# Thirteen raw weight buffers, new first and last norm chains, and 256 columns of each lo part on GpSimd

## The chip, the core and the metric

The kernel runs on one core of a Trainium2 chip. The metric is the device time of one execution in microseconds (us), lower is better. Engines are named as in the profile: PE (TensorE matmul), PEld (its weight loads), DVE (VectorE), ACT (ScalarE), POOL (GpSimd), SP (the queue that issues the DMAs).

## What is computed

A decoder trunk of two layers for 256 tokens of width 1024, in float32. Each layer is a token mixer (latent attention, retention, block attention behind one input projection), a layer norm, a channel mixer, and a layer norm; before the first layer stands one more norm. The channel mixer of layer 0 is a dense SwiGLU, that of layer 1 has eight experts, of which each token takes two:

```python
x = layer_norm(x, ln_emb_g, ln_emb_b)
for l in range(DEPTH):
    mix = hybrid_mixer(x, ...)
    x = layer_norm(DN_ALPHA * x + mix, ln1_g[l], ln1_b[l])
    f = swiglu(x, ...) if l % 2 == 0 else moe_swiglu(x, router, w_gate, w_up, w_down)
    x = layer_norm(DN_ALPHA * x + f, ln2_g[l], ln2_b[l])
# moe_swiglu, for each of 8 experts (D = 1024, inner width 3584):
y = y + gates[:, e:e + 1] * ((silu(xt @ w_gate[e]) * (xt @ w_up[e])) @ w_down[e])
```

## The kernel before

All weights are read once from HBM, 352 MB of them for the experts. To keep float32 accuracy at the speed of the rounded format fp32r, each weight tile `raw` is **split**: ACT writes `whi`, the tile rounded to fp32r (line 151), and DVE writes `wlo = raw - whi` (line 153). Activations are split in the same way, and a product is the sum of hi*hi, hi*lo and lo*hi.

The expert stage fills the last two thirds of the time. It goes over experts `e` (8) and blocks `m` of 512 inner columns (7). One such **m-step** reads three weight blocks (gate, up, and the down block of the m-step before) of two 128x2048 tiles each: six tiles of 1 MB, six splits. An expert that got more than 64 tokens (and expert 0 always) takes the branch `heavy`, with three matmuls for each 128x512 piece of weights; the others are **light**: tokens hi and lo lie side by side in one weight load, and two matmuls do for a piece. A `fold` matmul adds the two halves afterwards. Which branch is taken is known only when the kernel runs.

The tiles land in a ring of buffers: pools `raws`, `raws2` and `raws3` hold the counts of 0, 1 and 2 in `ORDER` (eleven in all), and piece number `EARLY` goes once into a borrowed tile. SP issues the DMA of a tile as soon as the buffer that it takes is free, which is when ACT and DVE have read its last content. `whi` and `wlo` have three buffers each in this stage. ACT and DVE run ahead of PE as far as these allow.

Between the splits DVE has small work that reads PSUM: `hh` (silu times up, line 938), `wk` (lo part of the turned hidden block, line 957), and now and then copies for gather and scatter. Their place in DVE's row is fixed by `defer`, which counts splits. POOL does almost nothing in this stage: it copies the rows of the last norm's scale and shift to all partitions (`gb`, line 1027) in expert 7.

At the very end the last down block runs, its result is scaled, scattered and added to the residual (`ln_sum`), and the last norm follows: sums on DVE and ACT, a handful of one-column operations on POOL (`ln_stats`, lines 187 to 195), then the rows of the result (line 202). At the very start scale and shift of the first norm are loaded by two DMAs that broadcast a row to 128 partitions (512 KB written each).

```python
            for c in range(0, 2048, n):
                ...
                split(raw(o + c, n), n, nc.vector, [x[:, c:c + n] for x in t])
                dve[0] = last[1]
```

Of the kernel before, what the change touches and what calls it, by code (L numbers as in the profile page):

```python
# [18 lines left out]
P = 128  # L19
# [15 lines left out]
EARLY = 11  # L35
# [7 lines left out]
WS = (8,3)  # L43
FENT = ((0, None, 2), (1, None, SPL))
ORDER = (0, 0, 0, 0, 1, 1, 1, 1, 0, 0, 2)
# [28 lines left out]
M_UT = M_E8 + 8  # L74
M_ON = M_UT + 128
M_ALL = M_ON + 128

# [9 lines left out]
def trunk(ctx: ExitStack, tc: tile.TileContext, x, consts, mconsts, vecs, lnrows, w_in, w_uq, w_ukv, w_o,  # L87
# [12 lines left out]
    mc = cpool.tile([P, M_UT], F32, name="mc")  # L100
# [4 lines left out]
    utb = cpool.tile([P, P], BF16, name="utb")  # L105
    onb = cpool.tile([P, P], BF16, name="onb")
# [77 lines left out]
    def ln_stats(s):  # L184
        nc.vector.tensor_scalar(s[:, 5:6], s[:, 0:1], s[:, 1:2], -1.0 / D, ALU.add, ALU.mult)
        nc.vector.tensor_scalar(s[:, 6:7], s[:, 1:2], s[:, 0:1], 1.0 / D, ALU.subtract, ALU.mult)
        nc.gpsimd.tensor_tensor(s[:, 6:7], s[:, 6:7], s[:, 6:7], ALU.mult)  # L187
        nc.gpsimd.tensor_scalar(s[:, 7:8], s[:, 3:4], 1.0 / D, LN_EPS, ALU.mult, ALU.add)  # L188
        nc.gpsimd.tensor_tensor(s[:, 7:8], s[:, 7:8], s[:, 6:7], ALU.subtract)  # L189
# [39 lines left out]
    def mixer(l, pool, poolb, cst, xhi, xlo, xres, raw, rest):  # L229
# [90 lines left out]
        if l == 0:  # L320
            load(cst, consts)
            load(mc[:, M_IO:], mconsts[:, M_IO:M_UT])
            uo = load(pool.tile([P, 2, P], F32, tag="oa", name="uo"), mconsts[:, M_UT:])
            nc.gpsimd.tensor_copy(utb, uo[:, 0, :])
            nc.gpsimd.tensor_copy(onb, uo[:, 1, :])
# [312 lines left out]
    def moe(pool, raws2, raws3, r, gb, rw):  # L638
# [28 lines left out]
        nc.gpsimd.tensor_copy(fo[:, :, 0], ident.rearrange("p (a b) -> p a b", b=2)[:, :, 1])  # L667
        for tt in range(2):
            ln_stats(r[tt][1])
        lgs = []  # L670
        for tt in range(2):
            x1 = ya[tt]
            pw, nm = ln_norm(*r[tt], gb, t0[:, tt], x1)
            lt = bank(acc, "lgp")
# [49 lines left out]
        iota = mc[:, M_IO:M_IO + 128]  # L724
# [150 lines left out]
        def gate_up(e, m, xg, part=None, mid=None):  # L875
# [60 lines left out]
            def mult():  # L936
                with after(dve[0]):
                    nc.vector.tensor_tensor(hh, bs[1], hh, ALU.mult)
# [5 lines left out]
            return hh, (lambda: fold_in(bs[1], fls[1])), mult  # L944

        def turn(hh, n, o=0):
# [5 lines left out]
            def halves():  # L952
# [3 lines left out]
                with after(dve[0]):  # L956
                    nc.vector.tensor_tensor(ht[:, :, 1], bv, ht[:, :, 0].bitcast(F32), ALU.subtract)  # L957
# [7 lines left out]
        def down(e, m, ht, yb, fold_up=None, fe=None, hook=None):  # L965
# [3 lines left out]

            def heavy(js=range(4)):  # L970
                for j in js:
                    for n in range(2):
                        cs = slice(j % 2 * D + n * 512, j % 2 * D + n * 512 + 512)
                        mm3(yb[n], ht[:, j, 0], ht[:, j, 1], sp[j // 2][0][:, cs], sp[j // 2][1][:, cs], m == 0 and j == 0, m == FM - 1 and j == 3)

            def light():
                for j in range(4):
                    if j == 3 and fold_up and fe == e:
                        fold_up()
                    h2 = ht[:, j].rearrange("p a b -> p (a b)")[:, 0:256:2]  # L980
                    for n in range(2):
                        for i in range(2):
                            nc.tensor.matmul(yb[n], h2, sp[j // 2][i][:, j % 2 * D + n * 512:j % 2 * D + n * 512 + 512],  # L983
                                             start=(m == 0 and j == 0 and i == 0), stop=(m == FM - 1 and j == 3 and i == 1))
# [167 lines left out]
        for e in range(NE):  # L1152
            pr = e // 2
            for m in range(FM):
# [29 lines left out]
        t1 = x3(F32, "t1", (P, 2, D))  # L1184
        for tt in range(2):
            ln_stats(fsums[tt])
# [250 lines left out]
```

## Time and profile before

| | before |
|---|---|
| time, median of 3 runs | 1436.97 us (1433.45 to 1437.19) |
| the profiled execution's own time | 1434.8 us |
| its span, first to last instruction | 1432.9 us |
| PE busy | 1355.6 us (95%) |
| DVE busy | 1171.8 us (82%) |
| ACT busy | 999.5 us (70%) |
| POOL busy | 68.3 us (5%) |
| read from HBM | 426.76 MB |

Busy shares are means over stages with different limits. The span is 1.9 us shorter than the time of the same execution. A PE that is busy all the time need not be at its peak, since the ends of matmuls are modelled.

### The profile page before, as it was taken

To read this page: it belongs to the slowest core of one execution; us is meant where nothing else is said; L and a number is where in the kernel's file an instruction comes from. 1 tells how busy PE (TensorE), PEld (TensorE's weight loads), DVE (VectorE), ACT (ScalarE), POOL (GpSimd) and SP (SyncE) were. 2 spreads that over 40 slices of the span, in tenths; PEclk is the share of its full clock that TensorE was granted. 3 is DMA by queue.
4 is the path that set the end of the run, shared out by engine and by line. 5 is a ranking of instruction groups with operands and counts; after the bars stand their busy time and mean duration, and the time that the engine had idled before them with its cause. 6 is when DMAs were issued, how large, how long until landed. Compare 5 with 4: busy or idle time off the path is not lost. (4 is left out here: it accounts for less than half of the span.)

```text
span 1432.9 us, 18660 instructions
## 1 busy us (share of the span) xinstructions
PE 1355.6 (95%) x6927; PEld 1121.2 (78%) x6927; DVE 1171.8 (82%) x1258; ACT 999.5 (70%) x1074; POOL 68.3 (5%) x110
## 2 busy tenths in 40 slices
PE   8999999999999899989989999999999999999994
PEld 7987999997987688867666678866678888886663
DVE  6577654557576988899999998889998888888996
ACT  4564444444564777788888887788887777778883
POOL 3011000003011000000000000000000000000101
PEclk9999999999999999999999999999999999999997
DMA  7733455453534689999999999999999999999980
GB/s 284 271 136 118 177 192 191 177 180 127 181 146 191 227 335 369 365 364 405 409 405 411 419 400 344 350 359 394 412 418 372 338 357 347 344 366 362 376 341 31
DMA packets 63515, 429.49 MB, mean 300 GB/s; under 512 B 7058, under 2 KB 7570, under 8 KB 15268
## 3 DMA queue, kind: packets, MB, share of 16 engines
q1 hardware_dynamic: 63364, 427.81, 77.7%
q8 instruction: 83, 1.36, 0.4%
q14 instruction: 36, 0.29, 0.1%
q0 software_dynamic: 32, 0.03, 0.0%
HBM read 426.76 MB, written 1.05 MB: 299 GB/s over the span
## 5 line engine op out<-in xcount | busy, mean ns | idle before, releaser
L153 DVE TENSOR_TENSOR wlo<-raw,whi 128x2048 fp32r<-128x2048 f32 (+5 forms) x479 | 917.1, 1935 | 163.8 <-ACT whi L151 161.7
L151 ACT CAST whi<-raw 128x2048 fp32r<-128x2048 f32 (+4 forms) x482 | 772.5, 1618 | 257.5 <-PE gu L586 43.9
L908 PE MATMUL eg<-wlo,xg 128*128 128x512 f32 x448 | 185.8, 415 | 17.9 <-DVE wlo L153 13.9
L162 PE MATMUL eg<-whi,xg 128*128 128x512 f32 x448 | 179.6, 401 | 0.0
L907 PE MATMUL eg<-whi,xg 128*128 128x512 f32 x448 | 178.7, 399 | 0.0
L163 PE MATMUL eg<-wlo,xg 128*128 128x512 f32 x448 | 177.7, 397 | 0.6 <-DVE wlo L153 0.3
L164 PE MATMUL eg<-whi,xg 128*128 128x512 f32 x448 | 176.9, 395 | 0.0
L908 PEld LDWEIGHTS eg<-wlo,xg 128*128 128x128 f32 x448 | 84.0, 187 | 68.0 <-DVE wlo L153 52.7
L163 PEld LDWEIGHTS eg<-wlo,xg 128*128 128x128 f32 x448 | 87.0, 194 | 19.4 <-DVE wlo L153 3.6
L983 PE MATMUL y<-whi,wk 128*128 128x512 f32 x224 | 90.8, 405 | 11.5 <-DVE wk L957 9.8
L164 PEld LDWEIGHTS eg<-whi,xg 128*128 128x128 f32 x448 | 87.0, 194 | 17.5
L585 PE MATMUL gu<-xhi,whi 128*128 128x256 f32 x352 | 99.8, 283 | 0.1
L586 PE MATMUL gu<-xlo,whi 128*128 128x256 f32 x352 | 99.7, 283 | 0.2 <-DVE xlo L225 0.2
L162 PEld LDWEIGHTS eg<-whi,xg 128*128 128x128 f32 x448 | 87.2, 195 | 16.0
L983 PE MATMUL y<-wlo,wk 128*128 128x512 f32 x224 | 93.3, 416 | 6.7 <-DVE wlo L153 5.5
L587 PE MATMUL gu<-xhi,wlo 128*128 128x256 f32 x352 | 99.6, 283 | 0.0
L907 PEld LDWEIGHTS eg<-whi,xg 128*128 128x128 f32 x448 | 84.3, 188 | 14.2 <-ACT whi L151 0.5
L162 PE MATMUL y<-whi,wk 128*128 128x512 f32 x224 | 87.4, 392 | 0.4 <-ACT hh L932 0.3
L163 PE MATMUL y<-wlo,wk 128*128 128x512 f32 x224 | 87.5, 391 | 0.2 <-DVE wlo L153 0.2
L164 PE MATMUL y<-whi,wk 128*128 128x512 f32 x224 | 87.3, 390 | 0.0
L585 PEld LDWEIGHTS gu<-xhi,whi 128*128 128x128 f32 x352 | 67.5, 192 | 0.7 <-DVE xlo L225 0.3
L586 PEld LDWEIGHTS gu<-xlo,whi 128*128 128x128 f32 x352 | 67.5, 192 | 0.6 <-DVE xlo L225 0.4
(317 smaller groups left out, 2071.8 us busy)
## 6 DMA issues: line engine op xcount, KB each, us to landing
raw<-in_e_gate SPq DMA_DIRECT2D x112, 1024.0 KB, 7.1
raw<-in_e_up SPq DMA_DIRECT2D x110, 1024.0 KB, 6.9
raw<-in_e_down SPq DMA_DIRECT2D x108, 1024.0 KB, 6.9
raw<-in_ffn_gu SPq DMA_DIRECT2D x22, 1024.0 KB, 4.9
raw<-in_ffn_dn SPq DMA_DIRECT2D x11, 1024.0 KB, 4.6
raw<-in_w_in SPq DMA_DIRECT2D x10, 960.0 KB, 4.6
raw<-in_w_o SPq DMA_DIRECT2D x8, 1024.0 KB, 6.7
gb<-in_lnrows SPq DMA_DIRECT2D x8, 512.0 KB, 5.7
```

What stands on the lines that cost most here:

```text
L151: last[0] = nc.scalar.copy(hi[:, :n], src)
L153: last[1] = (eng or nc.vector).tensor_tensor(lo[:, :n], src, hi.bitcast(F32)[:, :n], ALU.subtract)
L162: nc.tensor.matmul(o, ahi, bhi, start=start, stop=False)
L163: nc.tensor.matmul(o, ahi, blo, start=False, stop=False)
L164: return nc.tensor.matmul(o, alo, bhi, start=False, stop=stop)
L585: nc.tensor.matmul(o, hi[:, cs], xhi[:, k, :], start=(g == 0 and k == 0), stop=False)
L586: nc.tensor.matmul(o, hi[:, cs], xlo[:, k, :], start=False, stop=False)
L587: nc.tensor.matmul(o, lo[:, cs], xhi[:, k, :], start=False, stop=(g == 1 and k == 7))
L907: nc.tensor.matmul(bs[g], x2, sp[k // 4][0][:, cs], start=(k == 0), stop=False)
L908: nc.tensor.matmul(bs[g], x2, sp[k // 4][1][:, cs], start=False, stop=(k == 7))
L983: nc.tensor.matmul(yb[n], h2, sp[j // 2][i][:, j % 2 * D + n * 512:j % 2 * D + n * 512 + 512], start=(m == 0 and j == 0 and i == 0), stop= ...
```

## The change

Four things, in the order of the program:

1. **First norm.** The two rows of scale and shift (8 KB) are loaded to one partition, and PE multiplies them by a column of ones (four 128x512 float32 matmuls, `gbp`), so that they stand on all partitions in PSUM. DVE reads them there for the first 128 tokens; ACT copies them to SBUF for the others. The router's weights are loaded on SP at the start, and two constant matrices of the router are computed on DVE and POOL instead of loaded.
2. **Buffers.** `ORDER` has thirteen entries, with two more for `raws2`; the room comes from the constants and from a smaller scratch area for DMA descriptors.
3. **Side part.** For each full split of the expert stage (2048 columns, 326 of them) DVE subtracts the first 1792 columns, POOL the last 256.
4. **The end.** The last down block goes over its output halves one after the other (`order`) instead of alternating; of its four half splits the third lo part waits for `hh`, the fourth for `wk`; four float32 matmuls (`kw`) are added. The one-column operations of the last norm move from POOL to DVE, but for the power.

```diff
-EARLY = 11
+EARLY = 13
+WL = (2, 2)
+SIDE = 256
-ORDER = (0, 0, 0, 0, 1, 1, 1, 1, 0, 0, 2)
+ORDER = (0, 0, 0, 0, 1, 1, 1, 1, 1, 1, 0, 0, 2)
...
-    def split(src, n, lo_eng=None, to=None):
+    def split(src, n, lo_eng=None, to=None, side=0):
...
-            last[1] = (eng or nc.vector).tensor_tensor(lo[:, :n], src, hi.bitcast(F32)[:, :n], ALU.subtract)
+            h = n - side
+            if side:
+                nc.gpsimd.tensor_tensor(lo[:, h:n], src[:, h:n], hi.bitcast(F32)[:, h:n], ALU.subtract)
+            last[1] = (eng or nc.vector).tensor_tensor(lo[:, :h], src[:, :h], hi.bitcast(F32)[:, :h], ALU.subtract)
...
-                split(raw(o + c, n), n, nc.vector, [x[:, c:c + n] for x in t])
+                split(raw(o + c, n), n, nc.vector, [x[:, c:c + n] for x in t], SIDE if n == 2048 else 0)
...
                     def hook():
-                        mult()
+                        i = mult()
+                        kw = bank(wps, "kw")
+                        keep_warm(kw, mc, WL[0])
                         h2.append(turn(hh, 0, 1024))
+                        keep_warm(kw, mc, WL[1])
+                        hold_splits(((), None, 2), ((), None, 1, i), ((), None, 1, turned[0]))
...
         for tt in range(2):
-            ln_stats(fsums[tt])
+            s, t = st[tt], t1[:, tt]
+            ln_stats(s, nc.vector)
+            nc.vector.tensor_scalar(s[:, 8:9], s[:, 4:5], 1.0 / D, s[:, 7:8], ALU.mult, ALU.add)
+            nc.gpsimd.tensor_tensor(s[:, 9:10], s[:, 8:9], mhalf[:, :1], ALU.pow)
+            nc.vector.scalar_tensor_tensor(t, ya[tt], s[:, 5:6], g, ALU.add, ALU.mult)
...
-            t = gb_load(0)
-            gb = [t[i // 2][:, (i % 2) * 512:(i % 2 + 1) * 512] for i in range(4)]
+            rows = load(x3(F32, "rows", (P, 2, D))[0:1], lnrows[0:2, :].rearrange("(o a) b -> o a b", o=1))
             load(xin[1], x[P:S, :])
...
+                nc.tensor.matmul(gb[i], ones, rows[:, i // 2, cs], start=True, stop=True)
+                nc.scalar.copy(t[i // 2][:, cs], gb[i])
```

Three places in the order of instructions carry the prediction. First, DVE's row in expert 1, which is light in this run (`ys` and `r` are the scaled result and its scatter-add, the branches are those of `heavy` and `light`). Before:

```order
L153 TENSOR_TENSOR wlo<-raw,whi 128x2048 x2
L957 TENSOR_TENSOR wk<-ht,wk 128x4x128
L863 UNCONDITIONAL_BRANCH
L153 TENSOR_TENSOR wlo<-raw,whi 128x2048 x2
L997 UNCONDITIONAL_BRANCH
L863 UNCONDITIONAL_BRANCH
L153 TENSOR_TENSOR wlo<-raw,whi 128x2048 x2
L938 TENSOR_TENSOR hh<-eg,hh 128x512
```

The same place now, and behind it POOL's row, which was empty here:

```order
L156 TENSOR_TENSOR wlo<-raw,whi 128x1792 x2
L968 TENSOR_TENSOR wk<-ht,wk 128x4x128
L872 UNCONDITIONAL_BRANCH
L156 TENSOR_TENSOR wlo<-raw,whi 128x1792 x2
L1011 UNCONDITIONAL_BRANCH
L872 UNCONDITIONAL_BRANCH
L156 TENSOR_TENSOR wlo<-raw,whi 128x1792 x2
L947 TENSOR_TENSOR hh<-eg,hh 128x512
```

```order
L872 UNCONDITIONAL_BRANCH
L155 TENSOR_TENSOR wlo<-raw,whi 128x256 x2
L1011 UNCONDITIONAL_BRANCH
L155 TENSOR_TENSOR wlo<-raw,whi 128x256 x2
L872 UNCONDITIONAL_BRANCH
```

DVE's row keeps its order, with shorter lo parts, and POOL gets one instruction for each of them. In the four light experts 15 to 20 of 42 lo parts (36 in expert 7) are followed on DVE by at least one instruction that reads PSUM.

Second, POOL's row where it broadcasts the rows of the last norm in expert 7; the `ISA` rows without names set POOL up for the broadcast and back. Before, and now:

```order
L1027 ISA
L1027 ISA gb<-row 128x1024 x2
L863 UNCONDITIONAL_BRANCH x14
L174 ISA
L174 TENSOR_SCALAR sums<-sums 128x1 x2
```

```order
L155 TENSOR_TENSOR wlo<-raw,whi 128x256
L1041 ISA
L1041 ISA gb<-row 128x1024
L872 UNCONDITIONAL_BRANCH
L155 ISA
L155 TENSOR_TENSOR wlo<-raw,whi 128x256 x3
L872 UNCONDITIONAL_BRANCH
L1041 ISA
L1041 ISA gb<-row 128x1024
L155 ISA
L155 TENSOR_TENSOR wlo<-raw,whi 128x256 x2
```

The two broadcasts now stand between side parts, and POOL is set up four times there instead of once.

Third, DVE's row at the end (the last two down blocks, `hh` and `wk` of the last m-step, the scaling of `y`, the sums). Before, and now:

```order
L153 TENSOR_TENSOR wlo<-raw,whi 128x1024 x3
L938 TENSOR_TENSOR hh<-eg,hh 128x512
L153 TENSOR_TENSOR wlo<-raw,whi 128x1024
L957 TENSOR_TENSOR wk<-ht,wk 128x4x128
L863 UNCONDITIONAL_BRANCH
L1004 SCALAR_TENSOR_TENSOR wk<-y,gs,wk 128x512 x2
L181 SCALAR_TENSOR_TENSOR r,sums<-r,sc 128x512 x4
```

```order
L156 TENSOR_TENSOR wlo<-raw,whi 128x1024 x2
L947 TENSOR_TENSOR hh<-eg,hh 128x512
L156 TENSOR_TENSOR wlo<-raw,whi 128x1024
L968 TENSOR_TENSOR wk<-ht,wk 128x4x128
L156 TENSOR_TENSOR wlo<-raw,whi 128x1024
L872 UNCONDITIONAL_BRANCH
L1018 SCALAR_TENSOR_TENSOR wk<-y,gs,wk 128x512
L184 SCALAR_TENSOR_TENSOR r,sums<-r,sc 128x512
L1018 SCALAR_TENSOR_TENSOR wk<-y,gs,wk 128x512
L184 SCALAR_TENSOR_TENSOR r,sums<-r,sc 128x512 x3
```

`hh` moves ahead of one lo part, `wk` ahead of another, and the first scatter-add ahead of the second scaling. On PE the four `kw` matmuls stand ahead of the branch of the last down block but one.

## Rows read from the trace of the kernel before

**Rows 1.** Stretches: busy us of PE, PEld, DVE, ACT, POOL (instructions); PE clock; DMA share; GB/s.
```profile
16.00:20.00 4.00, 1.63 (x7) 1.27 (x8) 4.00 (x3) 1.46 (x2) 2.22 (x1) 0.94 1.03 432
...
520.00:600.00 80.00, 80.00 (x364) 66.63 (x363) 69.00 (x42) 58.12 (x41) 0.00 (x0) 1.00 0.93 357
650.00:800.00 150.00, 136.96 (x583) 100.50 (x582) 149.40 (x102) 132.72 (x114) 0.00 (x0) 1.00 1.01 408
```
**Rows 2.** DVE by line and shape, 520 to 600 us: count, busy us, mean ns, idle before.
```profile
L153 DVE TENSOR_TENSOR wlo<-raw,whi 128x2048 fp32r<-128x2048 f32 x28 | 64.1, 2292 | 11.3 <-ACT whi L151 11.3
```
**Rows 3.** The same, 650 to 800 us.
```profile
L153 DVE TENSOR_TENSOR wlo<-raw,whi 128x2048 fp32r<-128x2048 f32 x60 | 134.4, 2280 | 0.6 <-ACT whi L151 0.6
L938 DVE TENSOR_TENSOR hh<-eg,hh 128x512 f32<-128x512 f32 x10 | 6.8, 681 | 0.0
```
**Rows 4.** Waits of the DMA queue, 650 to 800 us: total us, times, longest.
```profile
SPq L120 <- DVE wlo L153: 120.6, 56, 3.7
```
**Rows 5.** Instructions in order of time, expert 2: start us, us, engine, what.
```profile
701.81 3.72 ACT L151 CAST whi<-raw 128x2048 fp32r<-128x2048 f32 x2
...
703.95 8.89 DVE L153 TENSOR_TENSOR wlo<-raw,whi 128x2048 fp32r<-128x2048 f32 x4
```
**Rows 6.** The same, first projection: DVE and POOL.
```profile
12.96 1.03 DVE L153 TENSOR_TENSOR wlo<-raw,whi 128x832 fp32r<-128x832 f32 x1
...
16.49 2.22 POOL L153 TENSOR_TENSOR wlo<-raw,whi 128x832 fp32r<-128x832 f32 x1 [0.67 <-ACT whi L151]
16.83 2.77 DVE L153 TENSOR_TENSOR wlo<-raw,whi 128x832 fp32r<-128x832 f32 x1
```
**Rows 7.** The same, rotary part of the first mixer: DVE and POOL.
```profile
66.44 1.15 DVE L153 TENSOR_TENSOR wlo<-raw,whi 128x960 fp32r<-128x960 f32 x1
66.61 1.59 POOL L453 TENSOR_TENSOR rqk<-rt 128x256 f32<-128x256 f32 x1 [32.05 <-DVE rt L451]
...
73.42 0.73 POOL L453 TENSOR_TENSOR rqk<-rt 128x256 f32<-128x256 f32 x1 [2.35 <-DVE rt L451]
...
73.47 0.42 DVE L398 CUSTOM_DVE_ANT_0 sm<-sc,cst 128x256 f32<-128x256 f32 x1
```
**Rows 8.** The same, POOL at the start, and its broadcast of the last norm's rows.
```profile
6.05 0.26 POOL L1258 TENSOR_SCALAR xmv<-xmv 128x1 f32<-128x1 f32 x1 [3.90 <-DVE xmv L1257]
...
1342.64 4.47 POOL L1027 PARTITION_BROADCAST gb<-row  x2 [872.52 <-PE sc L1011]
```
**Rows 9.** The same, the start: PE and DVE.
```profile
1.10 6.04 PE L208 MATMUL kw<-z 128*128 128x256 f32 x16 [1.10 <-POOL z L1239]
...
7.39 1.42 DVE L1267 SCALAR_TENSOR_TENSOR xr<-r,xmv,gb 128x512 f32<-128x512 f32 x2 [1.44 <-DMA gb<-in_lnrows]
...
19.66 0.71 PE L163 MATMUL pj<-wlo,xhi 128*128 128x416 f32 x1 [2.37 <-DVE wlo L153]
```
**Rows 10.** The same, the end.
```profile
1400.21 8.03 DVE L153 TENSOR_TENSOR wlo<-raw,whi 128x1024 fp32r<-128x1024 f32 x7
...
1408.16 0.68 DVE L938 TENSOR_TENSOR hh<-eg,hh 128x512 f32<-128x512 f32 x1
...
1408.89 1.12 PE L167 MATMUL ht<-mc,hh 128*128 128x128 f32 x4 [3.00 <-DVE hh L938]
...
1411.50 0.77 PE L983 MATMUL y<-whi,wk 128*128 128x512 f32 x1 [1.49 <-DVE wk L957]
...
1416.68 0.39 PE L983 MATMUL y<-whi,wk 128*128 128x512 f32 x1
...
1416.91 0.40 PE L983 MATMUL y<-wlo,wk 128*128 128x512 f32 x1
...
1420.77 0.68 DVE L181 SCALAR_TENSOR_TENSOR r<-r,sc 128x512 f32<-128x512 f32 x1
...
1428.16 1.42 DVE L202 SCALAR_TENSOR_TENSOR r<-t,sums,gb 128x512 f32<-128x512 f32 x2 [0.45 <-POOL sums L195]
```
**Rows 11.** Stretches at the end, columns as in rows 1.
```profile
1412.00:1416.00 4.00, 4.00 (x12) 3.11 (x11) 0.00 (x0) 0.00 (x0) 0.00 (x0) 0.56 0.00 0
```

More of the change, by code (lines that the diff above doesn't have):

```diff
@@ L321, in mixer @@
             load(cst, consts)
[L322 to L325, printed above, removed]
+            load(mc[:, M_IO:], mconsts[:, M_IO:M_ALL])
         proj_feat(IN_QK4, 1, 8, post_QK4)
@@ L667, in moe @@
         nc.gpsimd.tensor_copy(fo[:, :, 0], ident.rearrange("p (a b) -> p a b", b=2)[:, :, 1])
+        iota = mc[:, M_IO:M_IO + 128]
+        uo = pool.tile([P, 512], F32, tag="fl", name="uo")
+        ub = uo[:, 256:384].bitcast(BF16)
+        utb, onb = ub[:, 0:P], ub[:, P:2 * P]
+        nc.gpsimd.memset(onb, 1.0)
         for tt in range(2):
@@ L968, in down, with order @@
             sp = []
+            def order(js):
+                jn = [(j, n) for j in js for n in range(2)]
+                return sorted(jn, key=lambda x: x[1]) if (e, m) == (NE - 1, FM - 1) else jn
             def heavy(js=range(4)):
[L971 to L974, printed above, removed]
+                for j, n in order(js):
+                    cs = slice(j % 2 * D + n * 512, j % 2 * D + n * 512 + 512)
+                    mm3(yb[n], ht[:, j, 0], ht[:, j, 1], sp[j // 2][0][:, cs], sp[j // 2][1][:, cs], m == 0 and j == 0, m == FM - 1 and j == 3)
             def light():
-                for j in range(4):
-                    if j == 3 and fold_up and fe == e:
+                for j, n in order(range(4)):
+                    if (j, n) == (3, 0) and fold_up and fe == e:
                         fold_up()
                     h2 = ht[:, j].rearrange("p a b -> p (a b)")[:, 0:256:2]
[L981 to L984, printed above, removed]
+                    for i in range(2):
+                        nc.tensor.matmul(yb[n], h2, sp[j // 2][i][:, j % 2 * D + n * 512:j % 2 * D + n * 512 + 512],
+                                         start=(m == 0 and j == 0 and i == 0), stop=(m == FM - 1 and j == 3 and i == 1))
             if few[e] is not None:
@@ L1184, in moe @@
         t1 = x3(F32, "t1", (P, 2, D))
+        g, b = gb
+        st = fsums
         for tt in range(2):
[L1186 removed]
+            s, t = st[tt], t1[:, tt]
[3 more added lines that the diff above has]
+            nc.vector.scalar_tensor_tensor(t, ya[tt], s[:, 5:6], g, ALU.add, ALU.mult)
         for tt in range(2):
[L1188 removed]
+            for n in range(2):
+                cs = slice(n * 512, (n + 1) * 512)
+                nc.vector.scalar_tensor_tensor(ya[tt][:, cs], t1[:, tt][:, cs], st[tt][:, 9:10], b[:, cs], ALU.mult, ALU.add)
         return ya
@@ L1243, in start @@
             load(ident, mconsts[:, M_ID:M_ID + 128])
-            t = gb_load(0)
-            gb = [t[i // 2][:, (i % 2) * 512:(i % 2 + 1) * 512] for i in range(4)]
+            rows = load(x3(F32, "rows", (P, 2, D))[0:1], lnrows[0:2, :].rearrange("(o a) b -> o a b", o=1))
             load(xin[1], x[P:S, :])
+            ones = mp.tile([1, P], F32, tag="ones", name="ones")
+            nc.gpsimd.memset(ones, 1.0)
+            tg = x3(F32, "gb", (P, 2, D))
+            t = [tg[:, n, :] for n in range(2)]
+            gb = []
+            for i in range(4):
+                cs = slice(i % 2 * 512, i % 2 * 512 + 512)
+                gb.append(bank(acc, "gbp"))
+                nc.tensor.matmul(gb[i], ones, rows[:, i // 2, cs], start=True, stop=True)
+                nc.scalar.copy(t[i // 2][:, cs], gb[i])
             raw = win_a(0)
             load(vec, vecs)
+            load(rw, router)
             xhi, xlo = x3(F32R, "xhi"), x3(F32R, "xlo")
@@ L1319, in trunk @@
                     r = ffn(fp, *xx, nxt)
-    rw = load(cpool.tile([P, KD, NE], F32, tag="rw", name="rw"), router, nc.gpsimd)
     with tc.tile_pool(name="spl2", bufs=3, reuse_waits="tile") as spl[0], \
```

33 lines of the change are left out of this document (16 added, 17 removed).

## The prediction

> **What bounds the kernel now.** I read the stretches of the expert stage first, then DVE's groups and the waits inside them, and last the order of time at the places that the change touches.
>
> The expert stage has two regimes. In a heavy expert PE never pauses, 80.00 of 80 us, while DVE spends 11.3 us waiting for ACT [rows 1, 2]: 28 splits in 80 us are 2.86 us each, an m-step of six takes 17.1 us, and PE sets it. In light experts it is DVE that never pauses: 149.40 of 150 us, with 0.6 us of idle time ahead of its 60 lo parts [rows 1, 3]. There a split takes 2.50 us and an m-step 15.0 us. A lo part of 2048 columns takes 2280 ns, and four in a row take 8.89 us, so one follows the other every 2.22 us [rows 3, 5]; seven of 1024 columns take 8.03 us, 1.15 us each [rows 10]. A column of DVE work therefore costs (2.22 - 1.15) / 1024 = 1.05 ns. The DMA queue waits 120.6 of these 150 us for lo parts, which hold the buffers [rows 4]: the tiles are there, and DVE is late. But DMA isn't far behind: it moves 408 GB/s there, and 432 GB/s was the most that I saw, in a stretch at the start [rows 1]. ACT is busy 132.72 of the 150 us [rows 1].
>
> So a faster DVE would pay in four experts of eight and nowhere else in this stage; start and end are short chains of their own.
>
> **The change, part by part.**
>
> Side parts in light experts. DVE saves 256 columns, 256 x 1.05 = 0.27 us a split, 42 splits an expert: 11.3 us. Against it stands what POOL does to DVE. Where POOL subtracts 832 columns from 16.49 to 18.71, DVE's instruction of the same size takes 2.77 us instead of 1.03: it ends at 19.60, 0.89 us after POOL [rows 6]. Both read two operands from SBUF, and DVE stood still until POOL was done. The other way round, POOL's 256 columns take 0.73 us beside DVE instructions that read PSUM, which keep their time, but 1.59 us beside a lo part: they end at 68.20, 0.61 us after the lo part's end at 67.59 [rows 7]. So the two take turns, POOL gets its turn between two lo parts, and it holds DVE up only where DVE's next instruction reads two operands from SBUF.
>
> The price of one uncovered side part: POOL ends 0.61 us after the lo part ahead, and DVE's next ends 0.89 us after that where it would end 1.03 us after its start, with 0.06 us of overlap (2.28 against 2.22): 0.61 + 0.89 - (1.03 - 0.06) = 0.53, call it 0.5 us. A side part is covered where `hh`, `wk` or another reader of PSUM stands in that gap (`hh` takes 0.68 us [rows 3]); in the order that is 15 to 20 gaps of 42, which leaves 24. Sum for an expert: 24 x 0.5 - 42 x 0.27 = 12.0 - 11.3 = +0.7 us, and for four +3 us. The point from which it turns is 11.3 / 0.5 = 23 uncovered parts of 42. Bounds: with all 42 uncovered 21.0 - 11.3 = +9.7 us an expert, +39 us in all. With all covered DVE would need 15.0 - 1.6 = 13.4 us an m-step, but six tiles (6.29 MB) at 432 GB/s take 14.6 us, so 0.4 to 0.5 us a step can be had, 28 steps: -14 us. I take +3, since the rows show both the turn-taking and the cover.
>
> A rule speaks against this part: by the Trainium skill (SBUF — State Buffer, Who interferes with whom) a DVE instruction with two SBUF inputs and a POOL instruction that reads SBUF lock each other out, and the loser stands for the other's whole instruction. Rows 6 agree in kind. With POOL's whole 0.73 us as the price, the sum would be 24 x 0.73 - 11.3 = +6.2 us an expert, +25 in all; rows 6 and 7 show the lower price, because parts of both instructions overlap.
>
> Side parts in heavy experts. DVE with uncovered turns needs (0.5 - 0.27) x 6 = 1.4 us more an m-step at worst. It waits 11.3 us in 28 splits for ACT, 2.4 us an m-step, so it has the room: 0, with +14 us (0.5 us in each of 28 steps) as the upper bound, if PE starts to wait for late lo parts.
>
> Two more buffers. In neither regime does anyone wait for a tile, so they hide behind DVE and PE: 0. They would count only if DVE got faster than DMA.
>
> The broadcasts. The pair takes 4.47 us [rows 8] and was off every path. Now the side parts behind it wait, and PE and, three splits later, ACT and DVE with them. Slack of a split or so hides part: I take +2. What the set-up rows around it cost isn't seen. From above each is bounded by POOL's 3.90 us of idle time at the start, in which one stands too [rows 8]: 4 x 3.90 + 4.47 = +20; from below 0.
>
> By the Trainium skill (GPSIMD Engine Reference, 2.1 Instruction dispatch) the first call to a freshly loaded POOL kernel costs about 6 us that the profile doesn't show. If each of the four set-ups were such a load, an estimate from that page is 4 x 6 = 24 us, and the time 1457. No run so far shows it.
>
> Start. DVE waits 1.44 us for the broadcast rows and starts its norm at 7.39 [rows 9]. Now PE has first its eight `kw` matmuls, which end at 7.14 and take 0.755 us for 256 columns (sixteen records, two each) [rows 9]; four of 512 columns then take up to 6.0 us, the first half of the scale is there at 8.65 at the latest, the last of the shift at 13.2, and the norm of the first tokens ends more than 3 us later. For it, 1 MB less stands ahead of the weights, and PE's stall of 2.37 us at 19.66 [rows 9], where a lo part was shut out by POOL [rows 6], may go. I take 0, between -2.5 and +3. The router's three small DVE instructions lie in a wait for POOL: 0.
>
> End. `hh` comes one half lo part earlier, 1.15 us, at 1407.0. The four `kw` matmuls stand ahead of the block before, so PE's gap of 3.00 us ahead of the transposes [rows 10] closes; in the stretch behind that gap the granted clock was 0.56 on the mean [rows 11], most of it at the lower level of 1.2 GHz, and sixteen matmuls took from 1411.50 to 1417.3 = 5.8 us. At the full clock they start every 0.23 us [rows 10], 3.7 us: 2.1 less. With the halves one after the other, the sums of the first half run under the second: two of four, 1.1 us. On DVE the norm's small operations save the hops to POOL: the sums end at 1421.45, the rows at 1429.6 [rows 10], 8.1 us, of which some 7 stay (four halves of 0.71, two whole rows of 1.24, ten times 0.13 to 0.2, an estimate). 1.15 + 2.1 + 1.1 + 1 = 5.3: I take -5; if the clock falls all the same -2.5, at best -6.
>
> Sum against the profiled execution's own 1434.8 us (its span is 1432.9): 0 (start) + 3 + 0 + 0 + 2 - 5 (end) = **1435 us**, which is 0.1% under the median of 1436.97. By 0.3%, about 4.3 us, a measurement of this kernel can tell a time from no change, so this forecast is no change: what DVE gives up, its port takes back.
>
> **The rivals.**
>
> Slower: side parts miss the gaps. For the first of two tiles `whi` ends just ahead of its lo part: the pair of casts from 701.81 gives its first at 703.67, and the lo part starts at 703.95 [rows 5]. If POOL, which needs its own start-up, asks only after DVE has begun, its part comes behind the lo part, the wrong gap, and no part is covered: +39, with +2 and -5 that is 1471 us. It decides at 23 uncovered parts of 42; my 24 is on that edge. Against it: once DVE is held up, ACT gets further ahead, and POOL asks earlier.
>
> Faster: the gaps are used better than one for one, since a `hh` with a copy behind it covers longer than a part. DVE then falls under the DMA's 14.6 us a step, the two buffers carry the difference from heavy into light experts, and it is -14 + 2 - 5: 1418 us. Against it: 22 gaps of 42 have nothing in them, and someone must fill them.
>
> Slower by POOL's set-ups: +18 more in expert 7, 1453 us. For it: four of them stand between side parts. Against: nothing in the profile shows that they take long.
>
> The change doesn't do what it says at the end: the clock falls in the gap between the transposes and the first matmul, and the end gives 2.5 us: 1437.5, still no change.
>
> **How the numbers follow.** No change as worked out (with the last rival) 0.46, of which 0.15 end below the 0.3% and 0.06 above it, since 1435 lies 2 us under the median already; parts miss the gaps, wholly or in part, 0.25; gaps used better 0.19; set-ups 0.10. Faster: 0.19 + 0.15 = 0.34; same 0.46 - 0.15 - 0.06 = 0.25; slower 0.25 + 0.10 + 0.06 = 0.41. The likeliest case alone spans 1427 to 1443. The range goes to the faster rival with the better end, 1414, and up to 1468, most of the way to all parts uncovered.
>
> **What would show it.** Right: POOL's parts between lo parts, 0.6 us behind the end of one, and DVE's lo parts of 1792 columns in two groups, about 1.95 us and about 2.5 us, 2.50 us a split in the light stretch as before; DVE still without idle time there. For the faster rival: under 2.45 us a split, ACT or DMA waits in light experts. For the slower one: over 2.7 us a split, PE waiting for POOL. For the set-ups: a hole on PE near the broadcasts. For the end: a granted clock near 1 from `wk` to the last `y`, and some 5 us less from the last `hh` to the end. I would be wrong altogether if POOL's parts did not touch DVE, or if heavy experts got longer.

## The result, and the profile after

The changed kernel is slower: 1456.47 us, median of 4 runs (1454.34 to 1458.97), against 1435.21 us for the kernel before beside it; the ratio is 1.0158 with a 95% interval of 1.0140 to 1.0176. The profiled execution took 1454.34 us, its span is 1452.4 us. The forecast was no change, at 1435 us.

Where the 19.5 us between the two profiled spans lie is read off four marks that both traces have: DVE's first and last `ys` (the scaled results of experts 0 and 6), the last `hh` but one, and the end of the span.

| stretch | before, us | after, us | difference |
|---|---|---|---|
| start to the first `ys` | 619.90 | 615.39 | -4.5 |
| first to last `ys`, experts 1 to 6 | 698.56 | 698.28 | -0.3 |
| last `ys` to the last `hh` but one, expert 7 | 76.01 | 102.10 | +26.1 |
| that `hh` to the end | 38.43 | 36.63 | -1.8 |

The marks in order of time, of the kernel before and then of the changed one:

```profile
619.90 1.40 DVE L1004 SCALAR_TENSOR_TENSOR ys<-y,gs,ys 128x512 fp32r<-128x512 f32 x2
1318.46 1.40 DVE L1004 SCALAR_TENSOR_TENSOR ys<-y,gs,ys 128x512 fp32r<-128x512 f32 x2
1394.47 0.68 DVE L938 TENSOR_TENSOR hh<-eg,hh 128x512 f32<-128x512 f32 x1
```

```profile
615.39 1.39 DVE L1018 SCALAR_TENSOR_TENSOR ys<-y,gs,ys 128x512 fp32r<-128x512 f32 x2
1313.67 1.40 DVE L1018 SCALAR_TENSOR_TENSOR ys<-y,gs,ys 128x512 fp32r<-128x512 f32 x2
1415.77 0.68 DVE L947 TENSOR_TENSOR hh<-eg,hh 128x512 f32<-128x512 f32 x1
```

Experts 1 to 6 together hardly changed; expert 7 got 26.1 us longer. The -0.3 us hides two changes that cancel. From each expert's `ys` to the next, the light experts 1, 2 and 4 take 108.74, 108.41 and 108.44 us (108.56, 107.53 and 107.54 before), 2.0 us more; the heavy experts 3, 5 and 6 take 124.38, 126.07 and 122.24 us (125.24, 126.59 and 123.11 before), 2.2 us less. First the stage, with the same stretches as [rows 1] (columns as there):

```profile
520.00:600.00 80.00, 79.67 (x360) 65.94 (x358) 64.11 (x42) 58.05 (x40) 71.71 (x28) 1.00 0.94 359
650.00:800.00 150.00, 134.54 (x575) 100.23 (x575) 147.86 (x100) 132.31 (x110) 113.63 (x59) 1.00 1.00 408
1350.00:1400.00 50.00, 29.27 (x105) 22.06 (x106) 24.75 (x14) 26.14 (x20) 24.15 (x15) 0.76 0.60 231
```

In the heavy expert PE has 79.67 of 80 us, so late lo parts don't hold it. In the light ones 59 lo parts fit in the 150 us where 60 did before [rows 3]. The last row is the hole in expert 7: PE, DVE and ACT are each busy about half the time, and PE's granted clock is 0.76 on the mean (1.00 in the same stretch before). DVE's lo parts of the light stretch, by shape:

```profile
L156 DVE TENSOR_TENSOR wlo<-raw,whi 128x1792 fp32r<-128x1792 f32 x59 | 131.4, 2262 | 2.1 <-ACT whi L151 1.9
```

With an eighth of the columns gone, a lo part still takes 131.4 / 59 = 2.23 us (2.24 before [rows 3]): the time that DVE stands still for POOL is counted as busy. The sequence in order of time shows which ones pay:

```profile
639.90 2.01 DVE L156 TENSOR_TENSOR wlo<-raw,whi 128x1792 fp32r<-128x1792 f32 x1
641.84 0.67 DVE L1032 TENSOR_TENSOR r<-r,sc 128x512 f32<-128x512 f32 x1
642.43 4.49 DVE L156 TENSOR_TENSOR wlo<-raw,whi 128x1792 fp32r<-128x1792 f32 x2
646.85 0.68 DVE L947 TENSOR_TENSOR hh<-eg,hh 128x512 f32<-128x512 f32 x1
```

One between two readers of PSUM takes 2.01 us; two in a row take 4.49 us, so the gap between them costs. Now POOL around the two broadcasts of expert 7, in order of time (in brackets the idle time ahead):

```profile
1336.40 1.82 POOL L155 TENSOR_TENSOR wlo<-raw,whi 128x256 fp32r<-128x256 f32 x1 [0.71 <-DMA raw<-in_e_up]
1347.20 1.30 POOL L1041 PARTITION_BROADCAST gb<-row  x1 [8.97 <-issue]
1355.32 2.10 POOL L155 TENSOR_TENSOR wlo<-raw,whi 128x256 fp32r<-128x256 f32 x3 [6.82 <-issue]
1368.22 1.30 POOL L1041 PARTITION_BROADCAST gb<-row  x1 [10.79 <-issue]
1376.47 2.09 POOL L155 TENSOR_TENSOR wlo<-raw,whi 128x256 fp32r<-128x256 f32 x3 [6.95 <-issue]
```

A broadcast takes 1.30 us, but ahead of each POOL pauses for 8.97 and 10.79 us, and behind each for 6.82 and 6.95: 33.5 us in which it waited for nothing that the profile shows. What stands there in POOL's row are the set-up rows, and in two of the four places a branch. The loads of the two rows to broadcast were issued at 1310.5 and 1314.2 us, more than 30 us earlier. PE's idle times in the same place:

```profile
1345.29 0.89 PE L170 MATMUL ht<-mc,hh 128*128 128x128 f32 x4 [2.69 <-DVE hh L947]
1356.09 0.79 PE L917 MATMUL eg<-wlo,xg 128*128 128x512 f32 x1 [6.95 <-POOL wlo L155]
1377.24 0.80 PE L917 MATMUL eg<-wlo,xg 128*128 128x512 f32 x1 [13.66 <-POOL wlo L155]
```

PE stands still for 23.3 us, most of it for side parts that are queued behind a pause. The end, in order of time:

```profile
1428.32 0.68 DVE L947 TENSOR_TENSOR hh<-eg,hh 128x512 f32<-128x512 f32 x1
...
1431.20 0.77 PE L997 MATMUL y<-whi,wk 128*128 128x512 f32 x1 [1.49 <-DVE wk L968]
1431.77 0.63 PE L997 MATMUL y<-wlo,wk 128*128 128x512 f32 x1
1432.19 0.63 PE L997 MATMUL y<-whi,wk 128*128 128x512 f32 x1
...
1436.19 0.40 PE L997 MATMUL y<-wlo,wk 128*128 128x512 f32 x1
...
1441.64 0.19 ACT L179 ACTIVATION_READ_ACCUMULATOR jk<-r,sums 128x1 f32 x1
1441.97 1.27 DVE L1210 SCALAR_TENSOR_TENSOR t<-r,sums,gb 128x1024 f32<-128x1024 f32 x1
1443.17 0.15 DVE L191 TENSOR_TENSOR sums<-sums 128x1 f32<-128x1 f32 x1
...
1447.66 1.41 DVE L1214 SCALAR_TENSOR_TENSOR r<-t,sums,gb 128x512 f32<-128x512 f32 x2 [0.45 <-POOL sums L1209]
```

PE's gap of 1.49 us ahead of `y` is still there, and the first `y` follow each other by 0.43 us, the later ones by 0.23, as in [rows 10]. The gap of 3.00 us ahead of the transposes shrank to 1.22 us, and the transposes themselves take 0.66 us instead of 1.12.

### The profile page after: what moved, and what is told of

Its sections match the earlier page's. It is cut to its first block, busy times and chain, and to the rows that moved or that the text cites. A ratio compares the mean times of both kernels' runs of the same rounds, so it can differ in the third digit from the quotient of the medians.

```text
span 1452.4 us, 19509 instructions
## 1 busy us (share of the span) xinstructions
PE 1353.2 (93%) x6943; PEld 1125.2 (77%) x6943; DVE 1134.9 (78%) x1269; ACT 1002.6 (69%) x1078; POOL 786.9 (54%) x427
## 3 DMA queue, kind: packets, MB, share of 16 engines
HBM read 425.59 MB, written 1.05 MB: 294 GB/s over the span
## 5 line engine op out<-in xcount | busy, mean ns | idle before, releaser
L156 DVE TENSOR_TENSOR wlo<-raw,whi 128x1792 fp32r<-128x1792 f32 (+5 forms) x479 | 875.3, 1845 | 227.5 <-ACT whi L151 225.7
L155 POOL TENSOR_TENSOR wlo<-raw,whi 128x256 fp32r<-128x256 f32 x326 | 721.7, 2229 | 207.5 <-ACT whi L151 148.9
```

Source lines behind the costliest of these rows:

```text
L155: nc.gpsimd.tensor_tensor(lo[:, h:n], src[:, h:n], hi.bitcast(F32)[:, h:n], ALU.subtract)
L156: last[1] = (eng or nc.vector).tensor_tensor(lo[:, :h], src[:, :h], hi.bitcast(F32)[:, :h], ALU.subtract)
```

## The experiments

**Which part makes the hole.** Four kernels apart from the changed one: the rows of the last norm by DMA, no side parts, no side parts and the old buffers, and side parts alone on the kernel before.

```diff
 # a1_rows_dma, in ln_rows_bc2
...
-                load(rows[:, n], lnrows[8 + n:9 + n, :])
-                nc.gpsimd.partition_broadcast(o[:, n], rows[:, n])
+                load(o[:, n], lnrows[8 + n:9 + n, :].partition_broadcast(P))
 # a2_no_side (a3_no_side_11 also with the old ORDER and EARLY)
-SIDE = 256
+SIDE = 0
 # b1_side_only, in the kernel before, with SIDE and the split of the changed one
...
-                split(raw(o + c, n), n, nc.vector, [x[:, c:c + n] for x in t])
+                split(raw(o + c, n), n, nc.vector, [x[:, c:c + n] for x in t], SIDE if n == 2048 else 0)
```

> The changed kernel, with one difference: scale and shift of the last norm reach all partitions by two broadcasting DMAs instead of POOL's two PARTITION_BROADCAST, so that POOL does nothing but subtractions from the first expert to the last down block. Theory 1 (POOL's four pauses of 6.8 to 10.8 us around the broadcasts, with side parts queued behind each, make the hole of 26 us in expert 7): the pauses and the hole are gone, 1456 - 26 = 1430 us, 0.4% under the kernel before. Theory 2 (the broadcasts themselves hold the port, and the pauses run beside work that would have waited anyway): 2 x 1.3 us and little more come back, 1450 us or more. Theory 3 (side parts disturb expert 7 in another way, by its halved last blocks): the hole stays, 1456.

> The changed kernel without side parts (DVE subtracts all 2048 columns), with POOL's broadcasts left in. Theory 1: POOL's pauses are as long as in the changed kernel, but nobody is queued behind them, so the hole is gone: 1430 us, the same as with the rows loaded by DMA, since experts 0 to 6 took 699.2 us from the first scaled result to the last without side parts and 698.9 with them. If the side parts pay something that the seven experts' sum hides, this one is slower than the one with the rows by DMA, by up to 4 us.

> As the kernel without side parts, with eleven raw buffers as before: what is left of the change is the start, the end and the place of the router's constants. Theory 1, with buffers worth nothing since DVE and PE set the pace: the same as with thirteen, 1430 us, that is -5 (start) and -1.8 (end) against the kernel before, 1435 - 6.8 = 1428. Rival: the two buffers carry tiles from heavy into light experts, and without them it is 3 us or more slower.

> The kernel before with the side parts alone (256 columns of each full split on POOL). Theory 1: experts 0 to 6 as before, and the hole of about 26 us in expert 7: 1435 + 26 = 1461 us, ratio 1.018, with POOL idle 6 to 11 us ahead of each broadcast and behind it. Rival, that the hole comes from side parts together with the new end or the two buffers: 1435 us, no hole.

| kernel | us | ratio to before (95%) |
|---|---|---|
| rows by DMA | 1433.36 | 0.9999 (0.9984 to 1.0013) |
| no side parts | 1429.05 | 0.9969 (0.9954 to 0.9984) |
| no side parts, eleven buffers | 1429.42 | 0.9972 (0.9959 to 0.9984) |
| side parts alone | 1457.57 | 1.0168 (1.0143 to 1.0193) |

With the broadcasts gone or nobody behind them, 23 to 27 us come back; side parts alone bring the hole (last `ys` to the last `hh` but one takes 101.29 us there, against 76.01 before and 77.76 with the rows by DMA). Theory 1 holds, and the broadcast's own 1.30 us are not the matter. The stretch from the first to the last `ys` is 698.3 us with side parts and rows by DMA, and 698.3 without side parts; again light experts are longer with side parts (108.75, 108.36 and 108.45 against 108.57, 107.48 and 107.50 us) and heavy ones shorter. Why the heavy ones are shorter, no run here shows. Buffers are worth nothing while DVE has its full lo parts (1429.05 against 1429.42, within the intervals). The medians of rows by DMA and no side parts are 4.3 us apart. In their two profiles 1.7 us lie in expert 7 (77.76 against 76.05) and 1.3 at the end, where the clock fell in the one and not in the other (below); the first `ys` differs by 2.3 us the other way.

**What a turn of POOL to another kind of work costs.** One broadcast of 2048 columns in place of two of 1024:

```diff
-            for n in range(2):
-                load(rows[:, n], lnrows[8 + n:9 + n, :])
-                nc.gpsimd.partition_broadcast(o[:, n], rows[:, n])
+            load(rows, lnrows[8:10, :].rearrange("(o a) b -> o a b", o=1))
+            nc.gpsimd.partition_broadcast(o.rearrange("p a b -> p (a b)"), rows.rearrange("p a b -> p (a b)"))
```

> The changed kernel with one broadcast of 2048 columns in place of two of 1024, side parts kept: POOL turns to the broadcast once and back once, so there are two pauses instead of four. Theory 1 (each turn from subtractions to a broadcast or back costs POOL a pause of 7 to 11 us, whatever is broadcast): two pauses, about 9 and 7 us, PE stands still some 10 us where it stood 23, 1433 + 10 = 1443 us. Rival (the pauses grow with what is broadcast or wait for the rows' loads): the two pauses are longer, as long as the four together, 1456. Rival (a single turn is hidden by what DVE and PE have ready): 1435.

It took 1444.09 us, ratio 1.0065 (1.0043 to 1.0087), 10.7 us more than with the rows by DMA (9.5 by the two ratios, each to the kernel before beside it). POOL and PE in order of time:

```profile
1347.37 3.76 POOL L1040 PARTITION_BROADCAST gb<-row  x1 [7.35 <-DMA raw<-in_e_down]
1358.34 2.10 POOL L155 TENSOR_TENSOR wlo<-raw,whi 128x256 fp32r<-128x256 f32 x3 [7.21 <-issue]
...
1347.09 0.77 PE L170 MATMUL ht<-mc,hh 128*128 128x128 f32 x4 [2.71 <-DVE hh L947]
1359.11 0.79 PE L917 MATMUL eg<-wlo,xg 128*128 128x512 f32 x1 [8.27 <-POOL wlo L155]
```

Twice the columns, and no longer pause: two pauses of 7.35 and 7.21 us, PE idle 2.71 + 8.27 = 11.0 us. The profile puts the end of the first pause to the landing of a weight tile, but the broadcast doesn't read it, and the load of its own rows was issued at 1312.3. The cost goes by turns, not by what is broadcast.

**What a side part costs and what DVE could give.** In one kernel nobody does the last 256 columns, so DVE is freed and POOL does not touch it; in the other the side parts are 512 columns wide (the first has the POOL line of `split` removed, and PE reads the 256 columns ahead a second time in place of the missing ones, so that its work is the same; the second has the rows by DMA and `SIDE = 512`).

> What a freed DVE is worth without POOL's turns: the changed kernel without side parts, with DVE subtracting only 1792 of each 2048 columns and nobody the other 256. The lo parts of these 256 columns are left out; PE reads the 256 columns ahead of them in their place, so that its work is the same. Theory A, of the prediction (DVE sets the pace in light experts and DMA could go from 412 to 432 GB/s): a light m-step goes from 15.0 to 14.6 us, 1429 - 11 = 1418 us, and DVE waits for tiles. Theory B (DMA is at its limit in light experts already, at 412 GB/s, and DVE is only just as slow as it): 1429 us, the same as with full lo parts, and DVE idle some 8% of the light stretch. If B holds, the side parts could not have paid even without turns.

> The changed kernel with the last norm's rows by DMA and side parts of 512 columns instead of 256 (DVE 1536). Theory of turns (a side part with no reader of PSUM behind it adds its POOL time to DVE's row): covered splits shrink to 1.75 us, uncovered ones grow from 2.36 to some 2.5, POOL is busy all through light experts, which get longer: 1440 to 1460 us against 1433 with 256. If DVE had room behind DMA, or POOL's part cost DVE nothing: 1433 or less.

The first took 1401.51 us, ratio 0.9768 (0.9748 to 0.9789), the second 1469.20 us, ratio 1.0246 (1.0219 to 1.0273). The first one's light stretch, with the columns of [rows 1]:

```profile
650.00:800.00 150.00, 141.91 (x617) 108.91 (x616) 142.95 (x107) 140.42 (x119) 0.00 (x0) 0.99 1.01 418
```

Its lo parts in this stretch, by shape, and then two of them in a row, in order of time:

```profile
L154 DVE TENSOR_TENSOR wlo<-raw,whi 128x1792 fp32r<-128x1792 f32 x64 | 126.9, 2017 | 7.1 <-ACT whi L151 7.1
```

```profile
642.20 3.96 DVE L154 TENSOR_TENSOR wlo<-raw,whi 128x1792 fp32r<-128x1792 f32 x2
```

Two in a row take 3.96 us without POOL and 4.49 with it: one gap without a reader of PSUM costs 0.53 us, which is the price that the prediction worked out from [rows 6, 7]. (4.49 - 3.96 needs no model: it is the same pair in the same place.) Three in a row take 5.88 us, 1.96 each, against 2.22 for 2048 columns [rows 5]: 0.26 saved. The turns take back what the shorter lo part gives: (2.23 - 1.98) / 0.53 is 47%, so on the mean some 28 of 59 parts in the light stretch paid, an estimate; the prediction's turning point is 23 of 42, 55%. By the Trainium skill (SBUF — State Buffer, Who interferes with whom) the loser stands for the other's whole instruction; that would be 0.73 us, and the pairs show 0.53.

Theory A was right on the cause and short on the size: freed of 256 columns without turns, the kernel gains 27.5 us on the 1429.05 without side parts (28.8 by ratios), not 11. From `ys` to `ys` the light experts take 101.03, 101.59 and 101.47 us, where they take 108.57, 107.48 and 107.50 without side parts, and expert 7 up to its last `hh` but one takes 71.40 us against 76.05: 24.1 us in the four. A light m-step, a seventh of such a stretch, falls from 15.4 to 14.5 us. The 15.0 of the prediction came from the 60 lo parts that touch a window of 150 us, and some of them lie partly outside. An expert's 42 tiles of 1.05 MB in 101.0 to 101.6 us are 433 to 436 GB/s, while DMA brings 418 in the stretch shown: the rest must come out of the buffers, filled in the heavy experts. That is an account and not a test, since no run had the shorter lo parts with eleven buffers.

With 512 columns POOL's turn grows more than DVE's part shrinks: 55 lo parts in the same stretch, and the light experts take 117.9 to 118.6 us.

```profile
L156 DVE TENSOR_TENSOR wlo<-raw,whi 128x1536 fp32r<-128x1536 f32 x55 | 133.2, 2461 | 1.2 <-ACT whi L151 1.2
```

**The end.** Three matmuls that read `hh` stand in PE's gap, in place of two that could run ahead:

```diff
                         h2.append(turn(hh, 0, 1024))
-                        keep_warm(kw, mc, WL[1])
+                        keep_warm(kw, hh, 3)
```

> The changed kernel with the last norm's rows by DMA, and with the second two of the four kw matmuls replaced by three that read hh, so that they cannot run ahead of the block before and stand in PE's gap between the last transposes and the first y (1.49 us). Theory (the pause of PE lets the granted clock fall, and the first seven y then start 0.43 us apart): clock at the upper level through the last y, all sixteen y 0.23 us apart, the stretch from the last hh to the end 1.3 us shorter than with the rows by DMA alone, as it was in the kernel without side parts, where the clock happened to stay up; the time 1432, too little to be told by the runs. Rival (the fall is decided earlier, by PE's work before the gap): y as slow as before, or slower by the added matmuls.

> The kernel without side parts, with eleven buffers and POOL's broadcasts, and with kw in PE's gap ahead of the last y. Expected: the clock stays at the upper level through the end in every execution; 1429 us as without the gap's kw where the clock stayed up anyway, 1.3 us less where it fell: 1428 to 1429, ratio 0.997 to 0.995. If the clock had nothing to do with it: 1429.4 as measured without.

With side parts and rows by DMA: 1432.20 us, ratio 0.9986 (0.9970 to 1.0003); without side parts 1429.91 us, ratio 0.9971 (0.9957 to 0.9985). The time tells neither from its like without these matmuls. The trace does; of the first, in order of time:

```profile
1406.80 1.46 PE L212 MATMUL kw<-hh,mc 128*128 128x256 f32 x6
1408.46 0.48 PE L997 MATMUL y<-whi,wk 128*128 128x512 f32 x1 [0.20 <-DVE wk L968]
1408.78 0.39 PE L997 MATMUL y<-wlo,wk 128*128 128x512 f32 x1
1409.01 0.39 PE L997 MATMUL y<-whi,wk 128*128 128x512 f32 x1
```

All sixteen `y` now start 0.23 us apart but for the first, and the last `hh` to the last rows of `r` takes 17.87 us, against 19.20 with the rows by DMA alone: 1.33 us, as expected. But the theory isn't shown by that. Without these matmuls, with the same gap of 1.49 us, the first `y` were 0.43 us apart in six profiles (before and changed kernel, rows by DMA, side parts alone, the start alone, and DVE at 1792 columns) and 0.23 us apart in four (both without side parts, one broadcast, and 512 columns). With them they are 0.23 apart in three, and 0.43 in the fourth, the kernel of side parts where they are free, in order of time:

```profile
1390.11 0.66 PE L172 MATMUL ht<-mc,hh 128*128 128x128 f32 x4 [1.88 <-DVE hh L953]
1390.60 2.22 PE L214 MATMUL kw<-hh,mc 128*128 128x256 f32 x6
1392.26 0.99 PE L1003 MATMUL y<-whi,wk 128*128 128x512 f32 x1
1393.05 0.63 PE L1003 MATMUL y<-wlo,wk 128*128 128x512 f32 x1
```

There `kw` itself takes 2.22 us instead of 1.46, while the transposes ahead of it still take 0.66: the clock fell between the two, with 1.88 us of idle time ahead of the transposes. The price of the fall is shown (1.3 us), its cause is not. The first of PE's two pauses, ahead of the transposes, sorts the fourteen profiles in part. With 3.00 us there (the old end: before, side parts alone, the start alone) the clock fell in three of three; with 1.22 to 1.25 us and the second gap left open, in three of seven; with 1.87 to 1.88 us and `kw` in the second gap, in one of four. Seven profiles of fourteen had pauses of 1.2 us or more and no fall.

**The start alone.** The kernel without side parts, eleven buffers, and the old end:

> The new start alone (first norm's rows through PE, router's constants made on the chip) with the old end, old buffers, no side parts. In the profiles of the kernels with the new start the statistic after the first projection of the second tokens stands at 22.0 to 24.0 us against 24.4 before, depending on the clock of the first 12 us. Theory: the start is worth 0.4 to 2.4 us, the rest of the 4.4 us that the kernel without side parts gains is the end: 1432 to 1434 us against 1433 to 1434 before, ratio 0.998 to 1.000. Rival: the start brings all of it, ratio 0.997, and the end nothing.

1431.09 us, ratio 0.9982 (0.9967 to 0.9997): 0.18% or 2.6 us, with 0.4 to 4.7 in the interval. The old end in it takes 19.82 us from the last `hh` to the last rows of `r`, the new one 17.94 with the buffers and side parts alike, but the clock fell in the first and not in the second. Where it fell in both, the new end takes 19.20 (rows by DMA) and 19.34 (changed kernel), the old one 19.82 and 20.00. In the profile of the start alone the statistic after the first projection stands at 22.10 us; over all kernels with the new start it is at 22.0 to 22.3 or at 23.9 to 24.0, by how early the clock rises (the sixteen `kw` records at the start take 5.2 to 5.8 us in the first group and 6.0 to 6.6 in the second). With the old start it is at 24.39 before, and 25.8 with side parts alone. So of the 4.5 us at the first `ys`, 2.4 stand at this statistic, and the rest differs from execution to execution: the first `ys` lies between 613.7 and 621.2 us in the kernels with the new start.

**Side parts where they are free.** The side part is done only for splits whose lo part has a reader of PSUM behind it, and it waits for the lo part ahead; the second kernel leaves that wait out. Both have the rows by DMA and the `kw` in the gap. In the cut, `later` holds the deferred work, and `q[2]` says that it puts an instruction on DVE that reads PSUM.

```diff
...
+                cover = any(q[0] <= n // 1024 and q[2] for q in later)
-                split(raw(o + c, n), n, nc.vector, [x[:, c:c + n] for x in t], SIDE if n == 2048 else 0)
+                split(raw(o + c, n), n, nc.vector, [x[:, c:c + n] for x in t], SIDE if n == 2048 and cover else 0)
...
-                nc.gpsimd.tensor_tensor(lo[:, h:n], src[:, h:n], hi.bitcast(F32)[:, h:n], ALU.subtract)
+                i = nc.gpsimd.tensor_tensor(lo[:, h:n], src[:, h:n], hi.bitcast(F32)[:, h:n], ALU.subtract)
+                if last[1] is not None and any(k is last[1].ins for k in nc.cur_bb.bb.instructions):
+                    tc.add_manual_dep(i.ins, last[1].ins.name, mybir.DependencyInfo(mybir.DependencyClass.Sync, mybir.DependencyReason.DATA), reason="turn")
```

> Side parts only where they were free: the kernel with the last norm's rows by DMA and the kw in the gap, but a side part (256 columns) only for those full splits behind whose lo part DVE has an instruction that reads PSUM (hh, wk, a scaled result, a copy or an add of the gather and scatter), 128 of them in place of 326, some 16 in each expert, and each waits for the lo part ahead, so that POOL asks for its turn while the lo part with the reader behind it runs. Theory of turns (a side part costs 0.53 us in a gap without a reader and nothing in one with it, and saves 0.27 us of DVE): 16 x 0.25 = 4 us less in each light expert, four of them, 1432 - 16 = 1416 us, ratio 0.988; pairs of one 2048 and one 1792 lo part take 2.22 + 2.01 us. Rival (POOL's parts end after the reader, since they start up late): the next lo part is held up 0.2 to 0.3 us each time and the gain is gone, 1432 us. Rival (each part costs DVE a turn wherever it stands): slower than 1432.

> The same without the wait of each side part for the lo part ahead: POOL asks as soon as ACT's whi of the split is there. In light experts ACT ends whi one or two splits ahead of DVE, so theory of turns: POOL takes the gap one lo part too early, which has no reader, and a part costs 0.53 and saves 0.27: 16 x 0.26 = 4 us more in each light expert, 1432 + 16 = 1448 us, up to 32 us slower than with the wait. Rival (which gap POOL gets does not matter, or the natural time is the right one): the same time as with the wait.

With the wait: 1414.72 us, ratio 0.9863 (0.9842 to 0.9885), 1.4% faster than the kernel before, and faster than the changed one. Without it: 1432.45 us, ratio 0.9987 (0.9974 to 1.0000). The lo parts of 1792 columns in the light stretch, with the wait and then without:

```profile
L158 DVE TENSOR_TENSOR wlo<-raw,whi 128x1792 fp32r<-128x1792 f32 x24 | 49.2, 2051 | 0.5 <-ACT whi L151 0.5
```

```profile
L156 DVE TENSOR_TENSOR wlo<-raw,whi 128x1792 fp32r<-128x1792 f32 x24 | 56.4, 2352 | 0.3 <-ACT whi L151 0.3
```

With the wait a part costs 2.05 - 1.98 = 0.07 us and saves 0.26; from the first to the last `ys` it is 689.6 us instead of 698.3, and from there to the last `hh` but one 72.97 instead of 77.76 (76.05 without side parts). Against the kernel without side parts and with the same `kw`, 1429.91 us, the medians are 15.2 us apart, and in the profiles 11.9 us of it lie in the experts. One turn of it, POOL and DVE of the first kernel; the first line is the three lo parts ahead of `hh`:

```profile
653.10 6.45 DVE L158 TENSOR_TENSOR wlo<-raw,whi 128x1792 fp32r<-128x1792 f32 x3
657.85 2.31 POOL L155 TENSOR_TENSOR wlo<-raw,whi 128x256 fp32r<-128x256 f32 x1 [4.31 <-DVE wlo L158]
659.48 0.68 DVE L953 TENSOR_TENSOR hh<-eg,hh 128x512 f32<-128x512 f32 x1
```

POOL asks while a lo part runs, has its turn behind the end of that one at 659.55, and ends at 660.16, together with `hh`. Without the wait a lo part takes 2.35 us, 0.30 more than with it and 0.37 more than alone, which is more than the 0.26 that it saves. That was forecast as 0.53 for every part (1448 us). By the mean, 0.37 / 0.53 = 70% of the parts got a gap that has no cover, an estimate, not all. From `ys` to `ys` the light experts then take 109.66, 109.99 and 110.03 us, longer than with the side part in every split. The theory of turns is told from its first rival: it matters which gap POOL gets.

## Why the prediction was wrong

- **Side parts in light experts** (+3 taken): right, in mechanism and price. 0.53 us for a part without cover was measured as 0.53, 0.27 saved as 0.26. The light experts 1, 2 and 4 got 2.0 us longer, and expert 7 is 1.7 longer with side parts and without broadcasts (77.76 against 76.05): +3.7 where +3 was taken. The bound below, -14, was too small: 24.1 us were there in the four light experts. The step of 15.0 us that it starts from was read too short (15.4 over whole experts), and the step it ends at too long (14.6, against 14.5 with the shorter lo parts).
- **Heavy experts and buffers** (0): right for the buffers. The heavy experts 3, 5 and 6 got 2.2 us shorter, 0.5 to 0.9 each, where the sum has nothing. That this nearly cancels the light experts' 2.0 is luck, and its cause stays open.
- **The broadcasts** (+2 taken, +20 at most): this step failed. "From above each is bounded by POOL's 3.90 us of idle time at the start, in which one stands too": the four set-ups took 6.82 to 10.79 us, 33.5 us in all, and 26.1 us of it landed on the path, beyond even the bound. The row that bounded it was of another turn, at a time when POOL came from nothing. It was known that side parts were queued behind the pauses, and that a side part holds PE, DVE and ACT; "slack of a split or so" is then a few us against a pause of unknown length. In the kernel before, the profile could show nothing, because the broadcast had 872.52 us of idle time ahead of it [rows 8]. The rival "slower by POOL's set-ups", 1453 us, was the right one, and it had a chance of 0.10; its sign, a hole on PE near the broadcasts, is what the trace shows. By the Trainium skill (GPSIMD Engine Reference, 2.1 Instruction dispatch) a first call to a freshly loaded kernel costs about 6 us; its estimate was 1457 us. The runs agree that each turn costs, with 6.8 to 7.2 us on each way back, and 7.35 to 10.79 on the way to the broadcast. That this estimate came within 1 us of the 1456.47 measured is partly luck: the pauses are 33.5 us and not 24, and 26.1 of them reached the path. That the pause is a load, no run here shows.
- **The end** (-5 taken): right in its first term and wrong in the others, -1.8. `hh` came 13.69 - 12.55 = 1.14 us earlier (1.15 forecast). The `kw` matmuls did not close PE's gap ahead of the transposes but left 1.22 us of 3.00, and the transposes ran at the upper level: from `hh` to the first `y` 0.46 less. Then the clock fell all the same, the last rival: over the sixteen `y` 0.42 less, where 2.1 was forecast. The halves one after the other gave 0.43 from the last `y` to the last statistic (1.1 forecast), and the norm's small operations on DVE cost 0.65 where 1 was to be saved: the whole row `t` of the first tokens (1.27 us) stands in DVE's row ahead of the second tokens' operations, which POOL did beside it before.
- **The start** (0 taken): 0.4 to 2.4 us better than the profile before, and 2.6 by the runs of the start alone, at the good end of the bounds: the four broadcast matmuls take 3.69 us in the profile of the changed kernel, where 6.0 was the most.

## What to carry to other kernels

A row that bounds a cost must be of the same event: a pause between two kinds of work on GpSimd cannot be bounded by its idle time at the start, and a profile in which nobody waits for an engine says nothing on how long its set-ups take. Before work that others wait for is put on an engine that was idle, look at everything else in that engine's row; here two broadcasts of 1.30 us cost 26 us. Where two engines take turns, count what stands in the gaps and not the turns alone: the same side part cost 0.53 us in one gap and 0.07 in another, 128 parts at the wrong time cost more than 326, and choosing the gap and the time at which POOL asks made the change pay. A sum that comes out right over a stage can hide two errors; read it part by part.

## What the runs showed of the hardware

- A turn of POOL between TENSOR_TENSOR and PARTITION_BROADCAST paused it by 6.82 to 7.21 us on the way back (five of them: two in the changed kernel, 6.84 and 7.08 with side parts alone, one with one broadcast) and 7.35 to 10.79 us on the way there (five; 8.96 and 9.90 with side parts alone), with 1024 or 2048 columns. Three of the five on the way there the profile puts to the landing of a weight tile, which the broadcast doesn't read.
- DVE's subtraction of 1792 columns and POOL's of 256, both with two operands in SBUF, take turns: a POOL part between two of DVE's held DVE up by 0.53 us (4.49 against 3.96 us for the pair), and one beside an instruction of DVE that reads PSUM cost 0.07 us on the mean.
- Light experts used 433 to 436 GB/s of tiles for 100 us each, while DMA brought 418, out of thirteen buffers (with the shorter lo parts).
- At the end of the kernel, with PE pauses of 1.2 to 3.0 us and then 1.49 us, or with the second filled by matmuls, the granted clock was at the lower level of 1.2 GHz at the first `y` in seven profiles and at the upper one in seven. With 3.00 us in the first pause it was at the lower level in all three. The fall costs 1.3 us.
